# A mixture-of-experts kernel: experts of up to 64 tokens in a loop of their own, in plain float32 on two column groups

## Chip, cores and metric

One core of a Trainium2 chip. The metric is device time in microseconds for one execution, of the slowest core (here there is only one). Lower is better.

## What is computed

The kernel computes two transformer layers for 256 tokens of 1024 features, batch 1. The first layer has three attention branches; the second has a short convolution and a selecting attention, and then a mixture of experts, the part that matters here. With `t` the 256 tokens:

```python
scores = sigmoid(t @ w_router)                       # 256 x 64 experts
_, eidx = top_k(scores + router_bias, 8)             # 8 experts per token
g = take_along_axis(scores, eidx, axis=1)
g = g / sum(g, axis=-1) * 2.5
# for every expert e, over the tokens that chose it:
routed[tok] += (silu(t[tok] @ w1[e]) * (t[tok] @ w3[e])) @ w2[e] * g
out = routed + swiglu(t, ws1, ws3, ws2)
```

`w1` and `w3` are 1024 x 256 and `w2` 256 x 1024 for each of 64 experts, all float32: 2 MB for `w13` (w1 beside w3) and 1 MB for `w2` per expert. There are 256 x 8 = 2048 pairs of token and expert.

## The kernel before

Almost all matrix products keep float32 accuracy by splitting each operand into a high part that the fast float32 form (fp32r) holds exactly and a low part, and adding three products: high x high, low x high, high x low. The split costs one copy on ScalarE (high) and one subtraction on VectorE (low) per operand, weights included.

*Router* (`router`, L1324 to L1420). From the selection matrix `sel` (256 tokens x 64 experts) small products give the count per expert (`cnt`), a running start per expert and a slot number for each pair (`sg`, `sgT`), so that the 2048 slots hold the pairs sorted by expert. `nb` holds per expert whether it has a first block (count over 0.5) and a second one (over 128.5); `elist` lists, for each block, its expert and its first slot, `ecnt` the number of blocks. `place` (L1427) turns slot numbers into one-hot matrices. While the router's chain runs on VectorE, TensorE has the products of the shared expert.

*Gather* (`moe`, L1482 on). Four passes of 512 slots multiply the token rows with the one-hot matrices, so that `XT` holds the features of each slot and `ME` its expert weights and token number. The first blocks' weights are loaded and split meanwhile.

*The loop over blocks* (L1707 to L1755). A block is one expert with up to 128 slots, read at a start that is loaded into a register. Each iteration finishes block i - 1 and begins block i, with an order written out by hand for each engine:

- `stage_a(h, part)`: the first product, 128 slots as the stationary operand against w13 in halves h of 4 x 512 columns. Three products: 24 matmuls of 512 columns into `pa`.
- `silu`, `hidden`: silu(a) x b x gate into `ht`; `stage_t` transposes it in two pieces, `split_th` and `split_tl` split it.
- `stage_b(h)`: hidden x w2, three products: 12 matmuls of 512 columns into `py`; `split_yh` and `split_yl` split the result.
- `stage_c(h)`: adds the block's rows to their tokens, by a one-hot matrix `Q` (made from the token numbers by `token_distance` and `make_q`): 16 matmuls of 256 columns into the accumulators `acc`.
- `load_w` and `load_v`: six loads of 512 KB from SyncE's queue, for the next experts. SyncE first loads three expert numbers into registers.
- `split_wh`, `split_wl`, `split_vh`, `split_vl`: the splits of the weights on ScalarE, VectorE and, for one of them, GpSimd.

The loop runs from 1 to the number of blocks, which is known only at run time; the engines load it into registers (L1704). Behind the loop the last block is finished, the gate is applied and the output is stored (L1756 to L1775).

Of the kernel before, what the change touches and what calls it, by code (L numbers as in the profile page):

```python
# [20 lines left out]
S = 256  # L21
D = 1024
KD = 8
NE = 64
# [102 lines left out]
NSLOT = 2048  # L127
NB = 96
# [78 lines left out]
class Build:  # L207
# [1109 lines left out]
    def router(self, ps, lrow, r):  # L1317
        nc, a = self.nc, self.a
        rt = [self.s2("r"), self.s2("r"), self.s2("r", shape=(128, 512))]
        free = [r[:, t, s:s + 128].rearrange("p (a b) -> p a b", a=2) for r in rt[:2] for t in range(2) for s in (0, 128)]  # L1320
        w = lambda n: free.pop()
# [24 lines left out]
            nc.tensor.matmul(cps[:, 0:2], sel[:, qt, :], self.ones2, start=qt == 0, stop=qt == 1)  # L1346
        cnt = self.small([64, 2], F32, "cnt")
        nc.vector.tensor_copy(cnt, cps[:, 0:2])
        rk = self.pst([128, 2, NE], "O")
        nc.tensor.matmul(rk[:, 0, :], lt, sel[:, 0, :])  # L1350
        nc.tensor.matmul(rk[:, 1, :], self.ones2[:, 0:1].to_broadcast([128, 128]), sel[:, 0, :], start=True, stop=False)
# [13 lines left out]
        nb = self.small([64, 4], F32, "nb")  # L1365
# [4 lines left out]
        pps = self.pst([64, 4], "O")  # L1370
        nc.tensor.matmul(pps[:, 0:2], lt[0:64, 0:64], nb[:, 2:4])
        st = self.small([64, 4], F32, "st")
# [5 lines left out]
        self.places = [self.place(0)]  # L1378

        io = self.cm("iota")[0:64, 0:NB]  # L1380
        e1, e2 = rt[2][0:64, 0:NB], rt[2][0:64, 128:128 + NB]
        nc.vector.tensor_scalar(e1, io, st[:, 0:1], nb[:, 0:1], OP.is_equal, OP.mult)
        nc.vector.tensor_scalar(e2, io, st[:, 3:4], nb[:, 1:2], OP.is_equal, OP.mult)
# [12 lines left out]
        nc.tensor.matmul(nps, nb[:, 2:3], self.ones2[0:64, :])  # L1396
        self.ecnt = self.small([1, 2], I32, "ecnt")
        nc.vector.tensor_copy(self.ecnt, nps)
# [84 lines left out]
    def moe(self):  # L1483
# [4 lines left out]
        def tile(shape, dt, tag, bufs=1):  # L1488
            return mp.tile(shape, dt, tag=tag, name=tag, bufs=bufs)
# [116 lines left out]
        def meta_mm(b):  # L1606
            nc.tensor.matmul(pm[-1][:, 0:2], mslice, self.EB[:, bass.ds(b, 1), :].rearrange("p a b -> p (a b)"))
# [93 lines left out]
        nc.vector.tensor_scalar(zr, iota, 0.0, None, OP.mult)  # L1701
        for d2 in range(4):
            nc.tensor.matmul(acc2[d2], zr[:, 0:128], zr, start=True, stop=False, skip_group_check=True)
        n = nc.values_load(self.ecnt[0:1, 0:1], min_val=0, max_val=NB - 2)  # L1704


        with tc.For_i(1, n, 1, iteration_sync="reg_based") as iv:  # L1707
            with tc.manual_schedule():
# [44 lines left out]
                split_xl(1, s1)  # L1753
                load_w(0, e2, 0)
                split_wh(1, 1)  # L1755
        stage_t()  # L1756
        split_th()
        split_tl()
        token_distance()
        make_q()  # L1760
        for h in range(2):
            stage_b(h)
            split_yh(h)
            split_yl(h)
            stage_c(h)
# [29 lines left out]
```

## Time and profile before

| what | us |
|---|---|
| median of 3 runs | 998.45 (994.90 to 999.07) |
| the profiled execution | 997.92 |
| its span, from the first to the last instruction | 996.0 |
| TensorE busy (matmul) | 960.5 |
| VectorE busy | 809.0 |
| ScalarE busy | 599.9 |
| GpSimd busy | 162.2 |

Busy time counts the time in which at least one instruction of the engine was running. Matmuls overlap: one of 512 columns has a duration of 0.39 us, but the next one begins sooner; the distance of their starts is what one costs. The view by stretches gives for each engine its busy us and, in brackets, the number of instructions, then TensorE's granted clock (1.00 is full), the mean busy share of the 16 DMA engines, and what they moved. A timeline line gives start, duration, engine, line of the kernel, operation, what is written from what, shapes and how many instructions are merged into it; in square brackets stands how long the engine was idle before it and who ended that.

### The profile page before, as it was taken

How to read it: one execution, taken by the hardware profiler on the slowest of the kernel's cores; microseconds unless marked ns; L12 is line 12 of the kernel's file. 1: busy time of each engine (PE TensorE's matmuls, PEld its weight loads, DVE VectorE, ACT ScalarE, POOL GpSimd, SP SyncE). 2: the span in 40 equal slices, each digit the busy share in tenths (PEclk: the TensorE clock that was granted, in tenths of full speed). 3: DMA queues.
4: the chain of work that ended last, by engine and by line, in shares of the span. 5: the costliest groups of instructions: out<-in, count | busy, mean ns of one | idle time of the engine just before them, and what ended most of it. 6: DMA issues, size and time to landing. Idle time of an engine off the chain costs nothing. (4 is left out here: it accounts for less than half of the span.)

```text
span 996.0 us, 20282 instructions
## 1 busy us (share of the span) xinstructions
PE 960.5 (96%) x6666; PEld 884.2 (89%) x6666; DVE 809.0 (81%) x1479; ACT 599.9 (60%) x940; POOL 162.2 (16%) x111
## 2 busy tenths in 40 slices
PE   8999999999999999999898989999999999999996
PEld 7899999999999999999898977788888888888884
DVE  4777787777777758678874689799999999999994
ACT  5664654466355534555442535487887878878874
POOL 2311111011021000030200300021121221221211
PEclk9999999999999999999897989999999999999998
DMA  6576656676566465544330423388888888888884
GB/s 244 184 259 217 221 212 221 250 255 226 201 254 245 185 236 203 182 169 170 127 136 9 164 96 120 121 284 301 291 304 296 293 306 296 294 307 295 299 294 144
DMA packets 51209, 221.92 MB, mean 223 GB/s; under 512 B 5924, under 2 KB 6310, under 8 KB 41552
## 3 DMA queue, kind: packets, MB, share of 16 engines
q1 hardware_dynamic: 48960, 214.67, 60.9%
q0 software_dynamic: 1760, 5.42, 2.0%
q10 hardware_dynamic: 432, 1.05, 0.3%
q8 instruction: 38, 0.62, 0.3%
q14 instruction: 19, 0.16, 0.0%
HBM read 220.01 MB, written 1.11 MB: 222 GB/s over the span
## 5 line engine op out<-in xcount | busy, mean ns | idle before, releaser
L249 ACT ACTIVATE wh<-raw 128x2048 fp32r<-128x2048 f32 x75 | 143.5, 1914 | 108.5 <-DMA raw<-w_in 79.7
L250 DVE TENSOR_TENSOR raw<-raw,wh 128x2048 fp32r<-128x2048 f32 x75 | 171.5, 2287 | 14.8 <-ACT wh L249 14.6
L1536 ACT ACTIVATE wh<-raw 128x1024 fp32r<-128x1024 f32 x136 | 139.6, 1055 | 59.7 <-PE mm L1561 47.9
L329 PE MATMUL mm<-wh,hH 128*128 128x256 f32 x448 | 128.5, 287 | 0.0
L1545 POOL TENSOR_TENSOR raw<-raw,wh 128x1024 fp32r<-128x1024 f32 x32 | 77.0, 2407 | 302.3 <-PE mm L1561 302.3
L331 PE MATMUL mm<-wh,hL 128*128 128x256 f32 x448 | 125.9, 281 | 0.0
L330 PE MATMUL mm<-raw,hH 128*128 128x256 f32 x448 | 125.8, 281 | 0.0
L1560 PE MATMUL mm<-wh,xH 128*128 128x512 f32 x264 | 105.8, 401 | 0.0
L329 PE MATMUL mm<-hH,wh 128*128 128x256 f32 x352 | 103.1, 293 | 0.0
L1561 PE MATMUL mm<-wh,xL 128*128 128x512 f32 x264 | 103.0, 390 | 0.0
L331 PE MATMUL mm<-hH,raw 128*128 128x256 f32 x352 | 100.4, 285 | 0.9 <-DVE raw L250 0.9
L330 PE MATMUL mm<-hL,wh 128*128 128x256 f32 x352 | 99.9, 284 | 0.0
L329 PEld LDWEIGHTS mm<-wh,hH 128*128 128x128 f32 x448 | 84.5, 189 | 1.5
L330 PEld LDWEIGHTS mm<-raw,hH 128*128 128x128 f32 x448 | 84.5, 189 | 0.2 <-DVE raw L250 0.2
L331 PEld LDWEIGHTS mm<-wh,hL 128*128 128x128 f32 x448 | 84.4, 188 | 0.1
L1539 DVE TENSOR_TENSOR raw<-raw,wh 128x1024 fp32r<-128x1024 f32 x68 | 79.8, 1211 | 0.0
L1539 DVE TENSOR_TENSOR WL<-raw,wh 128x1024 fp32r<-128x1024 f32 x66 | 79.8, 1210 | 0.0
L598 DVE CUSTOM_DVE_ANT_0 ada<-ada,silc 128x1024 f32<-128x1024 f32 x48 | 58.6, 1221 | 24.9 <-DMA ada<-w_ada 24.9
L406 POOL TENSOR_TENSOR hr<-hss,mhalf 128x8 f32<-128x8 f32 (+2 forms) x24 | 41.8, 1743 | 169.0 <-DVE hss L405 168.8
L329 PEld LDWEIGHTS mm<-hH,wh 128*128 128x128 f32 x352 | 67.4, 191 | 1.1
L331 PEld LDWEIGHTS mm<-hH,raw 128*128 128x128 f32 x352 | 66.9, 190 | 1.2 <-DVE raw L250 1.2
L330 PEld LDWEIGHTS mm<-hL,wh 128*128 128x128 f32 x352 | 67.6, 192 | 0.0
(510 smaller groups left out, 2586.4 us busy)
## 6 DMA issues: line engine op xcount, KB each, us to landing
raw<-w SPq DMA_DIRECT2D x204, 512.0 KB, 5.4
raw<-w_in SPq DMA_DIRECT2D x58, 1024.0 KB, 4.8
ada<-w_ada SPq DMA_DIRECT2D x48, 512.0 KB, 5.8
raw<-w_out SPq DMA_DIRECT2D x8, 1024.0 KB, 4.7
raw<-w_branch SPq DMA_DIRECT2D x6, 1024.0 KB, 4.7
tb<-rext POOLq DMA_DIRECT2D x20, 256.0 KB, 4.7
raw<-ws SPq DMA_DIRECT2D x3, 1024.0 KB, 4.9
out<-x SPq DMA_DIRECT2D x4, 256.0 KB, 2.3
```

The source lines that it names most:

```text
L249: h = nc.scalar.activation(hi, raw, AF.Copy)
L250: l = nc.vector.tensor_tensor(lo, raw, hi, OP.subtract)
L329: nc.tensor.matmul(out, lh, rh, start=start, stop=False)
L330: nc.tensor.matmul(out, lh, rl, start=False, stop=False)
L331: self.last_mm = nc.tensor.matmul(out, ll, rh, start=False, stop=stop).ins
L406: nc.gpsimd.tensor_tensor(r, ss, self.mhalf[:, 0:2 * nh], OP.pow)
L598: nc.vector.tensor_tensor_reduce(raw, raw, self.silc, 0.5, 0.0, OP.mult, OP.add, self.ada[:, m:m + 1])
L1536: nc.scalar.activation(WH[h][:, half(p)], rw[h][:, half(p)], AF.Copy)
L1539: nc.vector.tensor_tensor(WL[h][:, half(p)], rw[h][:, half(p)], WH[h][:, half(p)], OP.subtract)
L1545: (nc.vector, nc.gpsimd)[f].tensor_tensor(VL[f], rw2[f], VH[f], OP.subtract)
L1560: nc.tensor.matmul(pa, xH[h][:, k, :], WH[h][:, ws], start=h == 0 and k == 0, stop=False)
L1561: nc.tensor.matmul(pa, xL[h][:, k, :], WH[h][:, ws], start=False, stop=False)
```

## The change

Experts with more than 64 tokens come first, in the first loop, which is as before. Those with 1 to 64 tokens come behind them in a second loop, two of them per iteration. There the weights are used as they are loaded, as plain float32, without a split. The stationary operand is 64 slots wide; the columns of w13 and of w2 are taken in two halves, one written to partitions 0 to 63 of the result and one to 64 to 127. The result of stage b lies in these two halves, so that stage c multiplies 64 rows at a time. The loads are 1 MB each instead of 512 KB. The router counts large and small experts and numbers the slots with the large ones first; the block that did the counting stands earlier. `ecnt` now holds the number of large blocks (at least 1) and the end of the second loop, and a second register load per engine reads it.

In the router (cut):

```diff
+        nc.vector.tensor_scalar(nb[:, 1:2], cnt[:, 0:1], 64.5, None, OP.is_gt)
+        nc.vector.scalar_tensor_tensor(q[:, 0:1], cnt[:, 0:1], 128.5, nb[:, 1:2], OP.is_gt, OP.add)
+        nc.vector.tensor_tensor(q[:, 1:2], cnt[:, 0:1], nb[:, 1:2], OP.mult)
+        nc.vector.scalar_tensor_tensor(q[:, 2:3], cnt[:, 0:1], 0.5, nb[:, 1:2], OP.is_gt, OP.subtract)
+        nc.vector.tensor_tensor(q[:, 3:4], cnt[:, 0:1], q[:, 1:2], OP.subtract)
+        pps = self.pst([64, 4], "O")
+        nc.tensor.matmul(pps, lt[0:64, 0:64], q, start=True, stop=False)
+        nc.tensor.matmul(pps[:, 2:4], self.ones2[0:64, 0:1].to_broadcast([64, 64]), q[:, 0:2], start=False, stop=True)
+        nc.vector.tensor_copy(pp, pps)
+        nc.vector.tensor_tensor(pp[:, 0:2], pp[:, 0:2], pp[:, 2:4], OP.subtract)
+        nc.vector.scalar_tensor_tensor(st[:, 0:2], pp[:, 0:2], nb[:, 1:2], pp[:, 2:4], OP.mult, OP.add)
...
-        nc.tensor.matmul(sb_ps, cnt[:, 0:1].to_broadcast([64, 128]), lt[0:64, 0:64])
+        nc.tensor.matmul(sb_ps, st[:, 1:2].to_broadcast([64, 128]), self.vec("ident")[0:64, 0:64])
...
-        nc.vector.tensor_scalar(nb[:, 0:1], cnt[:, 0:1], 0.5, None, OP.is_gt)
-        nc.vector.tensor_scalar(nb[:, 1:2], cnt[:, 0:1], 128.5, None, OP.is_gt)
-        nc.vector.tensor_tensor(nb[:, 2:3], nb[:, 0:1], nb[:, 1:2], OP.add)
-        nc.vector.tensor_copy(nb[:, 3:4], cnt[:, 0:1])
-        nc.tensor.matmul(pps[:, 0:2], lt[0:64, 0:64], nb[:, 2:4])
-        nc.vector.tensor_copy(st[:, 0:2], pps[:, 0:2])
```

The loops' bounds, and the products of the new loop (`part` are the partitions 0 to 63 and 64 to 127):

```diff
-        n = nc.values_load(self.ecnt[0:1, 0:1], min_val=0, max_val=NB - 2)
+        n = nc.values_load(self.ecnt[0:1, 0:1], min_val=1, max_val=NB - 16)
+        n_end = nc.values_load(self.ecnt[0:1, 1:2], min_val=1, max_val=NB - 16)
...
+        def s_a(pn, h, first, last):
+            w = W13[pn][h].rearrange("p (k g t c) -> p k g t c", k=4, g=2, t=2)
+            for k in range(4):
+                for t in range(2):
+                    nc.tensor.matmul(pa[part[t], 0:256], xs[pn][:, 4 * h + k, :], w[:, k, :, t, :],
+                                     start=first and k == 0, stop=last and k == 3)
...
+        def s_b(pn):
+            for f in range(2):
+                for t in range(2):
+                    c = 1024 * f + 512 * t
+                    nc.tensor.matmul(py[0][part[t], :], tS[pn][:, 64 * f:64 * f + 64], W2[pn][:, c:c + 512],
+                                     start=f == 0, stop=f == 1)
+
+        def s_c(pn):
+            for d in range(4):
+                ds = slice(128 * d, 128 * d + 128)
+                for y, last in ((yH[0], False), (yL[0], True)):
+                    for t in range(2):
+                        nc.tensor.matmul(acc[4 * t + d], y[part[t], ds], Qs[pn][part[t], :], start=False, stop=last,
+                                         skip_group_check=True)
```

One turn of the new loop (finishes expert i, begins i + 1), the piece between the loops, and the second loop. `s_load13` and `s_load2` issue the loads of 1 MB, `s_slot` loads a start slot into a register of VectorE, `s_x` copies 64 slots of `XT`, `s_meta` the weight and token numbers, `s_q` makes `Q`, `s_t` transposes the hidden values and `s_ts` copies them:

```diff
+        def s_turn(pc, i=None):
+            pn = 1 - pc
+            if i is not None:
+                e3, e2, s = expert(i + 3), expert(i + 2), s_slot(i + 2)
+            s_ts(pc)
+            s_a(pn, 0, True, False)
+            s_q(pn)
+            if i is not None:
+                s_load13(pn, 0, e3)
+                s_x(pc, i + 2, s)
+            s_b(pc)
+            split_yh(0)
+            if i is not None:
+                s_load2(pc, e2)
+            split_yl(0)
+            s_a(pn, 1, False, True)
+            if i is not None:
+                s_load13(pn, 1, e3)
+                s_meta(pc, i + 2)
+            s_silu()
+            s_hidden(pn)
+            s_c(pc)
+            s_t()
...
+            s_load13(0, 0, e0)
+            s_load2(0, e0)
+            s_load13(1, 1, e1)
+            s_load2(1, e1)
+            stage_t()
+            split_th()
+            split_tl()
...
+            s_a(0, 1, True, False)
+            s_load13(0, 1, e2)
+            stage_b(0)
...
+            stage_b(1)
...
+            stage_c(0)
+            stage_c(1)
+            s_a(0, 0, False, True)
+            s_load13(0, 0, e2)
+            s_silu()
+            s_q(0)
+            s_hidden(0)
...
+            s_t()
+        with tc.For_i(n, n_end, 2, iteration_sync="reg_based") as iv:
+            with tc.manual_schedule():
+                s_turn(0, iv)
+                s_turn(1, iv + 1)
+        with tc.manual_schedule():
+            s_turn(0)
+            s_ts(1)
+            s_b(1)
+            split_yh(0)
+            split_yl(0)
+            s_c(1)
```

The first loop's last iteration has already loaded one half of w13 for the first small expert and one for the second; the new loop takes these buffers over. The buffers of the split weights serve as the other float32 weight buffers.

## Rows read from the trace of the kernel before

**Rows 1.** The page: busy time of the engines, and the loads of the block loop.
```profile
PE 960.5 (96%) x6666; PEld 884.2 (89%) x6666; DVE 809.0 (81%) x1479; ACT 599.9 (60%) x940; POOL 162.2 (16%) x111
...
raw<-w SPq DMA_DIRECT2D x204, 512.0 KB, 5.4
```

**Rows 2.** Stretches: 50 us inside the block loop, and the last 16 us.
```profile
core 0: us, PE busy (x) PEld busy (x) DVE busy (x) ACT busy (x) POOL busy (x), PEclk, DMA share, GB/s
...
700.00:750.00 50.00, 50.00 (x270) 43.34 (x269) 48.97 (x73) 39.44 (x56) 12.04 (x5) 1.00 0.87 300
...
980.00:996.00 16.00, 8.40 (x30) 6.31 (x30) 3.86 (x8) 3.75 (x8) 2.17 (x3) 0.72 0.18 66
```

**Rows 3.** Timeline of SyncE's queue: the w13 loads of the last two iterations.
```profile
959.79 4.12 SPq L1504 DMA_DIRECT2D raw<-w  x4
...
970.32 4.12 SPq L1504 DMA_DIRECT2D raw<-w  x4
```

**Rows 4.** Timeline of TensorE inside one iteration: 512 columns, then 256.
```profile
805.93 1.08 PE L1563 MATMUL mm<-WL,xH 128*128 128x512 f32 x4
...
807.42 0.28 PE L1601 MATMUL S<-Q,hL 128*128 128x256 f32 x1
807.54 0.28 PE L1600 MATMUL S<-Q,hH 128*128 128x256 f32 x1
```

**Rows 5.** Timeline of TensorE in the second layer's attention: float32 on two row groups.
```profile
462.59 0.28 PE L331 MATMUL mm<-wh,hL 128*128 128x256 f32 x1
...
462.80 0.49 PE L1196 MATMUL S<-ki,qi 64*128 64x256 f32 x2
...
463.12 0.39 PE L1196 MATMUL S<-ki,qi 64*128 64x256 f32 x2
463.34 0.28 PE L1197 MATMUL S<-ki,qi 64*128 64x128 f32 x2
```

**Rows 6.** Groups of instructions by line and shape, 680 to 996 us: VectorE and ScalarE.
```profile
L1551 DVE TENSOR_SCALAR xH<-XT 128x512 fp32r x57 | 41.2, 723 | 0.0
...
L1595 DVE TENSOR_TENSOR hL<-O,hH 128x512 fp32r<-128x512 f32 x30 | 20.2, 674 | 0.0
L1592 ACT ACTIVATE hH<-O 128x512 fp32r<-128x512 f32 x29 | 17.4, 599 | 10.6 <-PE O L1589 10.6
...
L1569 DVE SCALAR_TENSOR_TENSOR ht<-th,meta,mm 128x256 f32<-128x256 f32 x29 | 13.9, 481 | 4.7 <-ACT th L1566 2.8
...
L1566 ACT ACTIVATE th<-mm 128x256 f32<-128x256 f32 x29 | 11.1, 383 | 6.2 <-PE mm L1563 6.1
```

**Rows 7.** Stretches: loads queued up at the start, and in the block loop.
```profile
7.50:15.00 7.50, 6.80 (x41) 6.31 (x42) 5.01 (x9) 6.07 (x13) 0.00 (x0) 0.77 1.01 410
...
954.00:956.50 2.50, 2.50 (x22) 2.42 (x21) 2.34 (x5) 1.97 (x4) 2.10 (x1) 1.00 0.99 395
940.00:970.10 30.10, 30.10 (x163) 26.09 (x162) 29.64 (x44) 23.69 (x35) 7.22 (x3) 1.00 0.87 292
```

**Rows 8.** Waits and timeline of TensorE at the loop's entry and exit.
```profile
PE O L1575 <- PEq L1707: 1.1, 1, 1.1
...
980.99 0.66 PE L1575 MATMUL O<-vecs,ht 128*128 128x128 f32 x2 [3.30 <-PEq L1784]
...
983.17 0.63 PE L1586 MATMUL mm<-wh,tH 128*128 128x512 f32 x1
...
987.30 0.39 PE L1589 MATMUL O<-raw,tH 128*128 128x512 f32 x1
...
989.93 0.28 PE L1601 MATMUL T<-Q,hL 128*128 128x256 f32 x1
```

**Rows 9.** Timeline of VectorE and TensorE in the router: count, slot starts, first slot product.
```profile
580.66 0.15 DVE L1348 COPY cnt<-O 64x2 f32<-64x2 f32 x1 [0.16 <-PE O L1346]
...
581.53 0.43 PE L1356 MATMUL O<-cmat,cnt 64*128 64x64 f32 x2
...
585.27 1.19 PE L1439 MATMUL O<-hH,sgT 64*128 64x512 f32 x2 [2.35 <-DVE mtH L1409]
```

More of the change, by code (lines that the diff above doesn't have):

```diff
@@ L1348, in router @@
         nc.vector.tensor_copy(cnt, cps[:, 0:2])
+        nb = self.small([64, 4], F32, "nb")
+        q = self.small([64, 4], F32, "nq")
+        nc.vector.tensor_scalar(nb[:, 1:2], cnt[:, 0:1], 64.5, None, OP.is_gt)
[6 more added lines that the diff above has]
+        nc.tensor.matmul(pps[:, 2:4], self.ones2[0:64, 0:1].to_broadcast([64, 64]), q[:, 0:2], start=False, stop=True)
+        pp = self.small([64, 4], F32, "pp")
+        nc.vector.tensor_copy(pp, pps)
+        st = self.small([64, 4], F32, "st")
+        nc.vector.tensor_tensor(pp[:, 0:2], pp[:, 0:2], pp[:, 2:4], OP.subtract)
+        nc.vector.scalar_tensor_tensor(st[:, 0:2], pp[:, 0:2], nb[:, 1:2], pp[:, 2:4], OP.mult, OP.add)
         rk = self.pst([128, 2, NE], "O")
@@ L1364, in router @@
         nc.scalar.activation(self.sgT, gps, AF.Copy)
-        nb = self.small([64, 4], F32, "nb")
-        nc.vector.tensor_scalar(nb[:, 0:1], cnt[:, 0:1], 0.5, None, OP.is_gt)
-        nc.vector.tensor_scalar(nb[:, 1:2], cnt[:, 0:1], 128.5, None, OP.is_gt)
-        nc.vector.tensor_tensor(nb[:, 2:3], nb[:, 0:1], nb[:, 1:2], OP.add)
-        nc.vector.tensor_copy(nb[:, 3:4], cnt[:, 0:1])
-        pps = self.pst([64, 4], "O")
-        nc.tensor.matmul(pps[:, 0:2], lt[0:64, 0:64], nb[:, 2:4])
-        st = self.small([64, 4], F32, "st")
-        nc.vector.tensor_copy(st[:, 0:2], pps[:, 0:2])
         nc.vector.tensor_tensor(st[:, 2:3], st[:, 1:2], cnt[:, 0:1], OP.add)
@@ L1378, in router @@
         self.places = [self.place(0)]
+        nc.vector.tensor_scalar(nb[:, 0:1], cnt[:, 0:1], 0.5, None, OP.is_gt)
+        nc.vector.tensor_scalar(nb[:, 2:3], cnt[:, 0:1], 128.5, None, OP.is_gt)
         io = self.cm("iota")[0:64, 0:NB]
@@ L1382, in router @@
         nc.vector.tensor_scalar(e1, io, st[:, 0:1], nb[:, 0:1], OP.is_equal, OP.mult)
-        nc.vector.tensor_scalar(e2, io, st[:, 3:4], nb[:, 1:2], OP.is_equal, OP.mult)
+        nc.vector.tensor_scalar(e2, io, st[:, 3:4], nb[:, 2:3], OP.is_equal, OP.mult)
         p2 = self.small([64, 4], F32, "p2")
@@ L1395, in router @@
         nps = self.pst([1, 2], "O")
-        nc.tensor.matmul(nps, nb[:, 2:3], self.ones2[0:64, :])
+        nc.tensor.matmul(nps, self.ones2[0:64, 0:1], q.rearrange("p (a b) -> p a b", b=2)[:, :, 0])
         self.ecnt = self.small([1, 2], I32, "ecnt")
-        nc.vector.tensor_copy(self.ecnt, nps)
+        en = self.small([1, 4], F32, "en")
+        nc.vector.tensor_copy(en[:, 0:2], nps)
+        nc.vector.tensor_tensor(en[:, 3:4], en[:, 0:1], en[:, 1:2], OP.add)
+        nc.vector.tensor_scalar(self.ecnt[:, 0:1], en[:, 0:1], 1.0, None, OP.max)
+        nc.vector.tensor_scalar(self.ecnt[:, 1:2], en[:, 3:4], -2.0, 1.0, OP.add, OP.max)
         nc.vector.tensor_tensor(G, sel, sa, OP.mult)
@@ L1755, in moe @@
                 split_wh(1, 1)
[L1756 to L1765, printed above, removed]
+        wh = self.turn["wh"]
+        f32t = lambda i: self.wp.tile([128, 2048], F32, tag=f"wh_{(wh + i) % 3}", name="wf", bufs=1)
+        W13 = [[f32t(1), rw[1]], [rw[0], f32t(2)]]
+        W2 = [rv, mp.tile([128, 2048], F32, tag="WL1", name="wf", bufs=1)]
@@ new lines, in moe, with s_load13 @@
+        xs = [tile([128, 4, 128], F32, f"xH{i}").rearrange("p a (b c) -> p (a b) c", b=2) for i in range(2)]
+        Qs = [Q, tile([128, 4, 128], F32R, "xL0")[:, 0:2, :].rearrange("p a b -> p (a b)")]
+        meta2 = [tile([128, 2], F32, f"meta2{i}") for i in range(2)]
+        tSS = tile([128, 2, 128], F32, "tH")
+        tS = [tSS[:, i, :] for i in range(2)]
+        ms = mslice
+        part = (slice(0, 64), slice(64, 128))
+        def s_load13(pn, h, e):
+            nc.sync.dma_start(W13[pn][h], a["w13"][bass.ds(e, 1), :, 2048 * h:2048 * h + 2048].rearrange("a p n -> p (a n)"))
@@ new lines, in s_load2, with expert, s_slot, s_x @@
+        def s_load2(pn, e):
+            nc.sync.dma_start(W2[pn], a["w2"][bass.ds(e, 1), :, :].rearrange("a p n -> p (a n)"))
+        def expert(i):
+            return nc.sync.value_load(self.elist[0:1, 0, bass.ds(i, 1)], min_val=0, max_val=NE - 1)
+        def s_slot(i):
+            return nc.vector.value_load(self.elist[0:1, 1, bass.ds(i, 1)], min_val=0, max_val=NSLOT)
+        def s_x(pn, i, s):
+            nc.vector.tensor_scalar(xs[pn], XT[:, :, bass.ds(s, 64)], 1.0, None, OP.mult)
+            for j in range(2):
+                nc.vector.tensor_scalar(ms[:, 64 * j:64 * j + 64], ME[:, bass.ds(s, 64)], 1.0, None, OP.mult)
@@ new lines, in s_meta, with s_q @@
+        def s_meta(pn, i):
+            meta_mm(i)
+            nc.vector.tensor_copy(meta2[pn], pm[-1][:, 0:2])
+        def s_q(pn):
+            nc.scalar.activation(pm[-1][:, 256:512], iota[:, 0:S], AF.Abs, bias=meta2[pn][:, 1:2], scale=-1.0)
+            nc.scalar.activation(Qs[pn], pm[-1][:, 256:512], AF.Relu, bias=1.0, scale=-1.0)
+        def s_a(pn, h, first, last):
[4 more added lines that the diff above has]
+                                     start=first and k == 0, stop=last and k == 3)
@@ new lines, in s_silu, with s_hidden, s_t, s_ts @@
+        def s_silu():
+            nc.scalar.activation(th[:, 0:128], pa[:, 0:128], AF.Silu)
+        def s_hidden(pn):
+            nc.vector.scalar_tensor_tensor(ht[:, 0:128], th[:, 0:128], meta2[pn][:, 0:1], pa[:, 128:256], OP.mult, OP.mult)
+        def s_t():
+            nc.tensor.transpose(py[1][:, 0:128], ht[:, 0:128], self.vec("ident"))
+        def s_ts(pn):
+            nc.vector.tensor_copy(tS[pn], py[1][:, 0:128])
+        def s_b(pn):
[4 more added lines that the diff above has]
+                                     start=f == 0, stop=f == 1)
@@ new lines, in moe @@
+        with tc.manual_schedule():
+            e0, e1, e2 = (expert(n + i) for i in range(3))
+            s0, s1 = (s_slot(n + i) for i in range(2))
+            s_load13(0, 0, e0)
[5 more added lines that the diff above has]
+            split_tl()
+            token_distance()
+            make_q()
+            s_x(0, n, s0)
+            s_meta(0, n)
+            s_a(0, 1, True, False)
[4 more added lines that the diff above has]
+            stage_b(1)
+            split_yh(1)
+            split_yl(1)
+            stage_c(0)
[5 more added lines that the diff above has]
+            s_hidden(0)
+            s_x(1, n + 1, s1)
+            s_meta(1, n + 1)
+            s_t()
@@ L1766, in moe @@
+        with tc.For_i(n, n_end, 2, iteration_sync="reg_based") as iv:
+            with tc.manual_schedule():
+                s_turn(0, iv)
+                s_turn(1, iv + 1)
+        with tc.manual_schedule():
+            s_turn(0)
+            s_ts(1)
+            s_b(1)
+            split_yh(0)
+            split_yl(0)
+            s_c(1)
         for p in range(KD // 2):
```

## The prediction, made before the changed kernel was run

> **What bounds the kernel now.** I read the page first, then stretches, then the loop over expert blocks, because the change lies in it. The page [rows 1] gives TensorE busy for 960.5 us, 96% of the span. The stretches [rows 2] show where room is left: in 700 to 750 us TensorE is busy 50.00 of 50 us at full clock and VectorE 48.97, while the DMA engines are busy 87% and move 300 GB/s; at the end (980 to 996) TensorE is busy only half the time and at a mean clock of 0.72. So the loop is bound by TensorE, with VectorE close behind; the loads are third.
>
> One iteration takes 10.53 us (the distance of the groups of w13 loads in [rows 3]). That is a sum of matmuls [rows 4]: 36 of 512 columns (four in a row take 1.08 us where one alone takes 0.39, so they start 0.23 us apart) and 16 of 256 columns (807.42 to 807.54, 0.12 us apart): 8.3 + 1.9 = 10.2 us, and two transposes and the meta product make up the rest. All of this is done for 128 slots, whatever the expert's own count.
>
> The trace doesn't show the counts. Evaluating the reference's router on its inputs gives 33 experts with tokens: 17 with 69 to 124, 16 with 1 to 59, none above 128. The trace agrees on the 33: 204 loads of 512 KB [rows 1] are 34 experts of 3 MB, one more than 33 because the loop loads ahead. So the first loop keeps 16 of its 32 iterations, 16 experts go to the new loop, and 16 x 10.53 = 168.5 us are taken out.
>
> **The change, part by part.** *TensorE in one turn of the new loop.* A float32 matmul is recorded as two matmuls. In [rows 5] two float32 matmuls of 64 rows and 256 columns stand side by side on the two row groups: the first two records begin at 462.80 and end within 0.49 us; the second two begin together at 463.12, and the next line begins at 463.34. So a record of 256 columns takes 0.22 us (463.12 to 463.34), a whole matmul 0.43 us, and the two groups run at the same time. The change pairs by columns instead: both halves read the same 128 partitions and write partitions 0 to 63 and 64 to 127. No row shows such a pair. Bounds: as parallel as the row groups (0.43 us a pair of 256 columns), or one after the other (0.86). I take the first, by the nearest rows, which are those row pairs. Then stage a is 8 pairs x 0.43 = 3.46 us, stage b 2 pairs of 512 columns x 0.86 = 1.73 us. Stage c is 16 matmuls of 64 rows in 8 pairs on row groups: 8 x 0.12 = 0.96 us (1.9 if they don't pair). The transpose and the two meta records take 0.35 us. Four times a turn the array changes its division; 462.59 to 462.80 [rows 5] is 0.21 us where 0.12 is usual, so 0.1 us each, and I take 0.6 us in all (0.4 to 1.2). Sum 7.1 us; ends 6.9 to 8.6.
>
> Nothing else in a turn is that long. VectorE has one 512-element copy (0.72 us), one split of y (0.67), the product (0.48) and four small ones, under 3 us; ScalarE has the y copy (0.60), silu (0.38) and the two for Q, under 2 us [rows 6]. All weight splits disappear. The chain stage a, silu, hidden, transpose costs 0.38 + 0.48 us and two handovers, some 1.1 us; it lies beside the meta product and stage c (1.4 us with the array changes), so I cost it at nothing; if that cover is gone it is 0.5 us a turn. The y splits (1.3 us) lie under the second half of stage a (1.73). On SyncE two register loads stand ahead of three issues, where one iteration had three ahead of six and kept up [rows 3]; a load is asked for over a turn before its use, so those queued behind a wait there have time. On VectorE the new register load stands ahead of the copy of the transposed hidden; stage b, which waits for that copy, has half a stage a (1.73 us) before it. I add 0.6 us a turn for waits that don't fit: **7.7 us a turn**.
>
> *Loads.* From the end of the first loop to the last w2 that is needed, 47 loads of 1.05 MB are issued: 49.3 MB. In the first loop 292 GB/s move at a share of 0.87 [rows 7], which would be 336 at a share of 1. Where the queue is backed up it is more: 410 GB/s in 7.5 to 15 us, with rows of 8 KB as the new loop has, and 395 GB/s for 2.5 us inside the loop [rows 7]. I take 385. The first new issue comes at about 979.5 us on the old time axis (the loop's last group of w13 is issued at 970.32 to 974.4 [rows 3]; then the loop's exit and three register loads). With 2 us to begin, the last w2 lands at 981.5 + 49.3 / 0.385 = 1109.5. TensorE asks for it at 1116.6 (below), so the loads are just covered; they end last below 49.3 / 135.1 = 365 GB/s. The Trainium skill gives a limit of about 358 GB/s of HBM bandwidth per core (DMA: Bandwidth & Descriptors, section Specifications). By it the loads would end last by 2.6 us and the sum would be 964; the 410 GB/s of [rows 7] speak against it.
>
> *The seams.* When the loop ends, TensorE stands still for 3.3 us, and then runs at half clock for some 6 us: a matmul of 512 columns takes 0.63 us at 983.17 and 0.39 again at 987.30 [rows 8], which is 0.43 against 0.23 us from one to the next. The change has two loops, so this comes twice; a loop's entry costs 1.1 us [rows 8]. Between the loops TensorE does, from 981.0 on: transposes 0.7, meta 0.4, half a stage a at half clock 3.5, 12 matmuls of stage b 3.3 (three of them at half clock), stage c 2.2 with its wait, the other half of stage a 1.7, silu, hidden and transpose uncovered 1.5, entry 1.1: 14.4 us. After the second loop: exit 3.3, the last turn 7.1 and 3.0 for the half clock, then stage b 1.7, y 1.3, stage c and array changes 1.2: 17.6 us. Before, the piece from 981.0 to the last matmul at 990.2 was 9.2 us [rows 8]; the output behind it is unchanged.
>
> *The router.* The block that counts large and small experts now stands ahead of the slot numbers. Five dependent VectorE operations of about 0.15 us (as the copy of the count), two small products and three more VectorE operations come between the count (580.66) and the product at 581.53 [rows 9]; the four operations and the product that stood later go. TensorE stands still 2.35 us before 585.27, waiting at the end of this VectorE chain [rows 9], so nothing covers what is added. Bounds: 0.5 us less (the later block is gone) to 2 us more; I take 0.9 us, by the length of the five operations, which is the nearest row. The second register load for the loop's end adds 0.5 us. Together 1.4 us.
>
> **Sum.** New: 14.4 + 14 x 7.7 + 17.6 = 139.8 us. Gone: 168.5 + 9.2 = 177.7 us. Difference 37.9, less 1.4: 36.5 us. Against the profiled execution (997.92 us, near the median of 998.45) that is **961 us**.
>
> **The rivals.** (a) *The column halves don't run side by side.* For it: both streams read the same 128 partitions, while those of [rows 5] read 64 each; a float32 record streams its operand for twice as long as a record of the split kind, so the way by which it comes in may not have room for two. Against it: a record of 256 columns takes 0.22 us, twice the 0.12 us of [rows 4], so one stream alone takes in columns at half the rate that those matmuls reach. Price: stages a and b double, 5.2 us a turn; the turn then has no slack and is 12.6 us; 14 x 4.9 + 13.9 for the seams and the last turn on top: **1044 us**. It decides from a pair that takes 1.45 times one matmul on (36.5 us over 16 turns is 2.3 us of 5.2): beyond that the change is slower.
> (b) *They overlap in part.* A pair that takes 1.25 times one matmul adds 1.3 us a turn, some 22 us in all: **983 us**. The Trainium skill gives 2.38 times for three column groups side by side (TensorE: Matmul & The Clock Gate, Part 3), where full overlap would be 3; an estimate from that page is a stretch of 1.26 and 984 us. No run here shows it.
> (c) *The loads stay at the rate they have now.* At 292 GB/s the last w2 lands at 1150, 34 us after it is wanted: **995 us**; at 336 GB/s it is 973 us. For it: the loop was never waiting for them, so nothing shows it sustained. Against it: [rows 7].
> (d) *The clock.* TensorE's clock fell to half after it stood still [rows 8]; if the waits of the new loop did that throughout, a turn would be over 14 us and the result over 1060 us. The waits that I expect are all under 1.5 us.
> That the change doesn't do what it says would mean fewer small experts than 16; each one fewer costs 2.8 us.
>
> **How the numbers follow.** Forecast with its own range of 947 to 974 us (a turn of 7.0 to 8.6 us, the seams 3 us better or worse): 0.70. Partial overlap, 974 to 1000 us: 0.10. Loads at the old rate: 0.04. Serial halves: 0.14. Clock: 0.02. The range 947 to 996 holds nearly all of the first, most of the second and the third: 0.8. A measurement of this kernel tells about 0.5% from no change (993 to 1003 us). Faster: the forecast, most of (b) and a little of (c), 0.80; same 0.05; slower 0.15.
>
> **What would show it.** After the change the first loop should have 16 iterations at 10.5 us. In the second, two float32 records of stage a should begin within some 0.02 us of each other, and pairs follow every 0.22 us; 0.22 us per single record would be rival (a). A turn should be 7 to 8.5 us; if TensorE's waits in it name the weights as what it waited for, the loads end last and their rate tells (c). After each loop there should be a pause of about 3 us and a half clock behind it. The router's wait before the first slot product should be within 2 us of 2.35. Wrong would be above all a different number of turns, or a pair that isn't one.

## The result, and the profile after

| what | us |
|---|---|
| before, median of 4 runs | 998.06 (994.90 to 999.07) |
| after, median of 4 runs | 966.39 (964.21 to 969.38) |
| ratio | 0.968, 95% interval 0.966 to 0.970 |
| after, the profiled execution | 969.38 |
| its span | 967.6 |

The change makes the kernel 31.7 us faster. Predicted were 961 us (947 to 996).

The page of the changed kernel, the lines that answer to [rows 1]:

```profile
PE 915.5 (95%) x6716; PEld 816.6 (84%) x6716; DVE 675.8 (70%) x1359; ACT 492.6 (51%) x812; POOL 124.0 (13%) x95
...
raw<-w SPq DMA_DIRECT2D x108, 512.0 KB, 5.2
wf<-w SPq DMA_DIRECT2D x25, 1024.0 KB, 10.0
...
raw<-w SPq DMA_DIRECT2D x23, 1024.0 KB, 9.6
```

The weight loads that were 204 of 512 KB are now 108 of 512 KB, 18 experts (17 large ones and one loaded ahead), and 48 of 1 MB. So the counts are as the prediction had them: 16 experts moved to the new loop. Each of the new loads needs 10 us from its issue to its landing, where those before needed 5.4 [rows 1]: the queue is backed up. The stretches show the same (columns as in [rows 2]):

```profile
700.00:750.00 50.00, 50.00 (x264) 43.12 (x263) 49.24 (x73) 39.89 (x58) 11.30 (x5) 1.00 0.89 299
...
860.00:900.00 40.00, 40.00 (x342) 24.73 (x340) 11.88 (x42) 10.44 (x24) 0.00 (x0) 1.00 1.01 422
900.00:930.00 30.00, 30.00 (x252) 17.93 (x248) 8.07 (x29) 6.95 (x16) 0.00 (x0) 1.00 1.01 422
930.00:945.00 15.00, 4.79 (x41) 2.85 (x37) 1.14 (x3) 0.88 (x2) 0.00 (x0) 0.71 0.99 414
945.00:967.00 22.00, 11.79 (x81) 6.59 (x81) 4.37 (x10) 3.65 (x8) 2.12 (x3) 0.81 0.14 50
```

The first loop (700 to 750) is as it was. In the second (860 to 930) TensorE is busy without a gap at full clock, VectorE and ScalarE have little to do, and the DMA engines are full: 422 GB/s at a share of 1.01. Both limits are reached at once. Then come 15 us with TensorE idle for 10 of them, while the loads go on at 414 GB/s, and a tail at a mean clock of 0.81. A gap of that size is the one large thing that the prediction did not have.

One turn of the new loop on TensorE, from the timeline (columns as in [rows 4]):

```profile
858.67 1.89 PE L1832 MATMUL mm<-wf,tH 128*64 128x512 f32 x8
860.39 1.90 PE L1813 MATMUL mm<-raw,xH 128*64 128x256 f32 x16
862.22 0.38 PE L1620 MATMUL O<-EB,mslice 66*128 x2
862.53 0.38 PE L1840 MATMUL S<-xL,hH 64*128 64x256 f32 x1
862.53 0.38 PE L1840 MATMUL T<-xL,hH 64*128 64x256 f32 x1
...
863.68 0.33 PE L1823 MATMUL O<-vecs,ht 128*128 128x128 f32 x1
863.93 1.95 PE L1813 MATMUL mm<-raw,xH 128*64 128x256 f32 x16
865.71 1.89 PE L1832 MATMUL mm<-raw,tH 128*64 128x512 f32 x8
```

Stage b (L1832) begins at 858.67 and again at 865.71: a turn of 7.04 us. Half a stage a (L1813) is 8 matmuls, recorded as 16; they take 860.39 to 862.22, 1.83 us, so two records every 0.23 us. Taken record by record (the single records behind a merged line), the two column groups begin 0.007 us apart, and pairs follow every 0.216 us. Stage c (L1840) shows its row pairs openly: two records at 862.53.

The seams, from the same timeline:

```profile
817.58 0.66 PE L1588 MATMUL O<-vecs,ht 128*128 128x128 f32 x2 [3.05 <-PEq L1929]
...
819.79 0.56 PE L1620 MATMUL O<-EB,mslice 66*128 x2 [1.56 <-DVE mslice L1799]
...
832.60 0.35 PE L1620 MATMUL O<-EB,mslice 66*128 x2 [1.39 <-DVE mslice L1799]
...
834.21 3.51 PE L1813 MATMUL mm<-raw,xH 128*64 128x256 f32 x16 [1.09 <-ACT O L1806]
...
934.67 0.33 PE L1823 MATMUL O<-vecs,ht 128*128 128x128 f32 x1
946.74 3.52 PE L1813 MATMUL mm<-raw,xH 128*64 128x256 f32 x16 [11.74 <-PEq L1929]
...
955.50 1.94 PE L1832 MATMUL mm<-wf,tH 128*64 128x512 f32 x8 [0.38 <-DVE tH L1826]
```

The first loop ends with a pause of 3.05 us, like the 3.30 of [rows 8]. The second ends with one of 11.74 us: the last turn in the loop is over at 935.0, and TensorE, VectorE and ScalarE begin again together at 946.72 to 946.74. What follows runs at half clock first (granted clock 0.50 from 946.7 to 950.0; 3.52 us for 16 records that take 1.90 inside the loop).

What TensorE waits for is not named: "PEq" is its own sequencer. The waits of SyncE's queue name it. First 930 to 960 us of the changed kernel, then its first loop's end (805 to 820), then the loop's end of the kernel before (960 to 985), a row that I had not read (columns: who waits and for whom, us in total, times, longest):

```profile
SPq L1900 <- DMA wf<-w: 7.3, 3, 2.5
SPq L1900 <- DMA raw<-w: 4.5, 2, 2.4
```

```profile
SPq L1721 <- DMA raw<-w: 3.4, 3, 1.4
```

```profile
SPq L1707 <- DMA raw<-w: 4.0, 3, 1.5
```

L1900, L1721 and L1707 are the lines of the loops themselves. At a loop's end SyncE waits for each load that is still in flight, and no engine goes on before SyncE does. Behind the second loop these are five loads, with a landing every 2.48 us (1.05 MB at 422 GB/s): 7.3 + 4.5 = 11.8 us, the length of TensorE's pause. Before, it was three shorter waits for loads of 512 KB, 4.0 us; record by record the last of these loads is seen at 980.34, SyncE is through at 980.9, and TensorE begins at 980.99 [rows 8]. The pause that I took for a fixed price of a loop's end was already mostly a wait for loads.

### The profile page after: what moved, and what is told of

Read it like the earlier page. It is cut to its first block, busy times and chain, and to the rows that moved or that the text cites. A ratio compares the mean times of both kernels' runs of the same rounds, so it can differ in the third digit from the quotient of the medians.

```text
span 967.6 us, 19260 instructions
## 1 busy us (share of the span) xinstructions
PE 915.5 (95%) x6716; PEld 816.6 (84%) x6716; DVE 675.8 (70%) x1359; ACT 492.6 (51%) x812; POOL 124.0 (13%) x95
## 3 DMA queue, kind: packets, MB, share of 16 engines
q10 hardware_dynamic: 432, 1.05, 0.3%
## 5 line engine op out<-in xcount | busy, mean ns | idle before, releaser
L331 PE MATMUL mm<-hH,raw 128*128 128x256 f32 x352 | 100.8, 286 | 1.6 <-DVE raw L250 1.6
L1549 ACT ACTIVATE wh<-raw 128x1024 fp32r<-128x1024 f32 x72 | 73.6, 1055 | 35.0 <-PE mm L1574 28.3
L1608 DVE TENSOR_TENSOR hL<-mm,hH 128x512 fp32r<-128x512 f32 x33 | 22.5, 683 | 62.3 <-ACT hH L1605 62.3
L1558 POOL TENSOR_TENSOR raw<-raw,wh 128x1024 fp32r<-128x1024 f32 x16 | 38.6, 2412 | 171.2 <-PE mm L1574 171.2
L490 ACT ACTIVATE sp<-sp,am 128x256 f32<-128x256 f32 x96 | 42.3, 443 | 27.1 <-DVE am L470 27.1
L1573 PE MATMUL mm<-wh,xH 128*128 128x512 f32 x136 | 54.4, 400 | 0.0
L1574 PE MATMUL mm<-wh,xL 128*128 128x512 f32 x136 | 53.1, 391 | 0.0
```

Of the source, the lines that this page charges most:

```text
L331: self.last_mm = nc.tensor.matmul(out, ll, rh, start=False, stop=stop).ins
L490: nc.scalar.activation(p, p, AF.Exp, bias=m[:, qt, G - 1:G], scale=-1.0, accum_out=s[:, half, qt, g:g + 1])
L1549: nc.scalar.activation(WH[h][:, half(p)], rw[h][:, half(p)], AF.Copy)
L1558: (nc.vector, nc.gpsimd)[f].tensor_tensor(VL[f], rw2[f], VH[f], OP.subtract)
L1573: nc.tensor.matmul(pa, xH[h][:, k, :], WH[h][:, ws], start=h == 0 and k == 0, stop=False)
L1574: nc.tensor.matmul(pa, xL[h][:, k, :], WH[h][:, ws], start=False, stop=False)
```

## The experiments

The theory after the result: (1) the column groups run at the same time, and because of that a turn is 7.05 us; (2) the pause behind the second loop is the backlog of loads; (3) the large loads hold 422 GB/s, and this just covers TensorE; (4) so the change has a fixed price for its seams and a gain per small expert. Each was set against a rival. The kernel before ran beside the experiments at 997.93 to 999.84 us, as the median of each call.

**Same column group.** Both halves go to partitions 0 to 63, added up there:

```diff
-                    nc.tensor.matmul(pa[part[t], 0:256], ...
-                                     start=first and k == 0, stop=last and k == 3)
+                    nc.tensor.matmul(pa[same[t], 0:256], ...
+                                     start=first and k == 0 and t == 0, stop=last and k == 3 and t == 1)
...
-                    nc.tensor.matmul(py[0][part[t], :], ...
+                    nc.tensor.matmul(py[0][same[t], :], ...
```

> The changed kernel with one edit: both column halves of stages a and b of the small experts go to partitions 0 to 63, so to one column group, and are added up there (so the output of these experts is not the wanted one; the work, its operands and its order are the same). Nothing can run side by side in these two stages. The theory, that the two column groups give a factor of two in these stages, expects that a pair of records of 256 columns then takes 0.43 us where it takes 0.216, a turn 7.05 + 3.46 + 1.73 = 12.2 us, that the loads then have slack and the wait at the second loop's exit falls below 4 us, and in all 966 + 14 x 5.2 + 12 (the piece between the loops, the last turn) - 8 (the exit) = about 1043 us, slower than the kernel before. The rival, that one column group alone takes in the next matmul early enough to hide part of it, expects turns of 8 to 10 us and 980 to 1010 us.

Measured: 1038.2 us (one run), a turn of 12.2 us. Its timeline of TensorE, and the wait at the second loop's exit:

```profile
860.99 3.60 PE L1833 MATMUL mm<-raw,tH 128*64 128x512 f32 x8
864.42 3.62 PE L1814 MATMUL mm<-wf,xH 128*64 128x256 f32 x16
867.97 0.38 PE L1620 MATMUL O<-EB,mslice 66*128 x2
```

```profile
PE mm L1814 <- PEq L1930: 4.4, 1, 4.4
```

The same 16 records take 864.42 to 867.97, 3.55 us instead of 1.83, and the turn is 5.15 us longer, of which 5.2 were expected. This is the price that the prediction gave for serial halves (1044 us), here in a run. So the second column group is worth 5.15 us a turn and decides the sign of the whole change: without it the kernel is 40 us slower than before. With a turn of 12.2 us the loads have slack, and the exit's pause falls to 4.4 us.

**No pairs in the order.** The two halves of stages a and b stand one behind the other instead of alternating:

```diff
-            for k in range(4):
-                for t in range(2):
+            for t in range(2):
+                for k in range(4):
```

(and in stage b the loops over `f` and `t` likewise)

> The two column halves of stages a and b are issued one after the other (all matmuls to partitions 0 to 63, then all to 64 to 127), same arithmetic. Theory (halves run side by side when they are issued in turn, 0.22 us per pair of records): pairs disappear, each turn gets 5.2 us longer (7.05 to 12.2 us), the loads then have slack and the wait at the second loop's exit falls from 11.7 to about 4 us; in all about 79 us more than the changed kernel, 1045 us. Rival (the records only look paired, the array works on one at a time): order makes no difference, 966 us.

Measured: 979.26 us (one run), a turn of 8.1 us: neither. Its timeline of TensorE:

```profile
857.82 2.21 PE L1813 MATMUL mm<-wf,xH 128*64 128x256 f32 x13
859.66 0.64 PE L1832 MATMUL mm<-wf,tH 128*64 128x512 f32 x1
859.87 0.59 PE L1813 MATMUL mm<-wf,xH 128*64 128x256 f32 x2
860.14 0.59 PE L1832 MATMUL mm<-wf,tH 128*64 128x512 f32 x1
860.30 0.38 PE L1813 MATMUL mm<-wf,xH 128*64 128x256 f32 x1
860.51 1.45 PE L1832 MATMUL mm<-wf,tH 128*64 128x512 f32 x5
```

Stage a (L1813) and stage b (L1832), which follow each other in the program, are mixed here. Record by record, the second group's first matmul begins at 858.736, when three of the eight records of the first group are still to come, and the first group's last one begins at 859.378 (which group a record belongs to is told by its distance to the next, 0.216 us). So by the profile's start times TensorE takes matmuls of the other column group ahead of those that are still waiting for their own, but not without limit: 1.03 us of the possible 5.15 is lost a turn. The pairs come from the column groups; the order only has to keep the two halves near each other. Fifteen turns of 1.03 us are 15.5 us; the exit's pause is 3.6 us shorter, since the loads have more time, and 966.4 + 15.5 - 3.6 = 978 fits the 979:

```profile
PE mm L1813 <- PEq L1929: 8.1, 1, 8.1
```

**No loads in the loop.** All loads inside the second loop are left out:

```diff
-                e3, e2, s = expert(i + 3), expert(i + 2), s_slot(i + 2)
+                s = s_slot(i + 2)
...
-                s_load13(pn, 0, e3)
...
-                s_load2(pc, e2)
...
-                s_load13(pn, 1, e3)
```

> The loads inside the second loop are left out (the experts from the 20th on are computed with weights of the experts before them). Theory (a turn is bound by TensorE, the exit by loads in flight): turns stay at 7.05 us, the exit falls from 11.7 us to 3 us or less; 957 us. Rival (turns are bound by the loads): turns fall below 6.8 us, 952 us or less.

Measured: 951.09 us (one run). The exit of its second loop, from the timeline of TensorE:

```profile
928.69 0.33 PE L1823 MATMUL O<-vecs,ht 128*128 128x128 f32 x1
929.54 1.95 PE L1813 MATMUL mm<-raw,xH 128*64 128x256 f32 x16 [0.53 <-PEq L1925]
```

Without loads the pause is 0.53 us where it was 11.74, and no half clock follows (1.95 us for the 16 records). The turns stay at 7.04 us: inside the loop the loads cost TensorE only some 0.6 us, in the last two turns (7.19 and 7.47 us in the changed kernel). The turn around the exit takes 7.3 us instead of 20.1, 12.8 us. So the mechanism is the theory's; its size is larger than I expected, because the half clock went with the pause. That the total is at 951 and not at 969.38 - 12.8 = 956.6 has a cause ahead of the change: the profiled execution of the changed kernel reaches the first loop some 5 us later than this one (its first block's transpose stands at 645.6 us, here at 640.6).

**Written out.** The second loop's 14 turns are written out for this input's counts, so there is no second loop, and the two loads that nobody uses are left out (diff cut):

```diff
-        with tc.For_i(n, n_end, 2, iteration_sync="reg_based") as iv:
-            with tc.manual_schedule():
-                s_turn(0, iv)
-                s_turn(1, iv + 1)
         with tc.manual_schedule():
+            for i in range(17, 31):
+                s_turn((i - 17) % 2, i)
             s_turn(0)
```

> The second loop's 14 turns are written out one after the other for this input's counts, and the two loads that nobody uses (w13 of a 34th expert) are left out; no loop exit between the turns. Theory (at the exit of a loop SyncE waits until every load in flight has landed, and all engines wait for SyncE; the weights that the next turn needs are there already): the 11.7 us at the exit and about 1 us of the half clock behind it disappear, 954 us. Rival (the last weights end last anyway, the exit only shows it): only the 5 us of the two unused loads are saved, 961 us.

Measured: 952.39 us (951.25 to 954.30), ratio 0.952 (0.951 to 0.954). The end of its turns, from the timeline of TensorE:

```profile
929.39 1.95 PE L1813 MATMUL mm<-raw,xH 128*64 128x256 f32 x16 [0.18 <-DMA raw<-w]
...
936.84 1.95 PE L1813 MATMUL mm<-wf,xH 128*64 128x256 f32 x16 [0.19 <-DMA wf<-w]
```

All loads are there, at 420 GB/s, and TensorE waits 0.2 us for two of them. So the 11.74 us behind the loop were no need of the computation: the weights for the last turn were there in time, and only the loop's end asked for more. This run takes away the loop's end and the two unused loads (5 us of the queue) together; the run with late loads, next, has no unused loads but keeps the loop, and its pause is still 5.8 us. Relative to the kernel before, this version is 15.8 us faster than the changed kernel (47.5 against 31.7). From 20.1 to 7.1 us around the exit is 13.0 us of it, and 9.7 to 7.0 in the first turn, without the loop's entry and its half clock, is 2.7; one of its turns takes 8.1 us and gives 1.1 back (TensorE waits 0.82 us for VectorE's split there; why in this turn alone, I don't know). It is the fastest version that does all the work, but for these counts alone: the number of turns is fixed in the program.

**Late loads.** The w13 of the expert after next is asked for at the turn's start, into the buffer that has just come free, instead of one turn ahead in halves; so there are fewer loads in flight, and none that nobody uses:

```diff
-                e3, e2, s = expert(i + 3), expert(i + 2), s_slot(i + 2)
+                e2, s = expert(i + 2), s_slot(i + 2)
+                s_load13(pc, 0, e2)
+                s_load13(pc, 1, e2)
...
-                s_load13(pn, 0, e3)
...
-                s_load13(pn, 1, e3)
```

> w13 of expert i + 2 is asked for at the beginning of turn i instead of w13 of expert i + 3 in its course, so that at the exit only loads that are used are in flight, and fewer. Theory (the exit waits for what is in flight): the exit falls from 11.7 to about 6 us, turns grow from 7.2 to at most 7.5 us since they now wait for loads at 422 GB/s; 962 to 966 us. Rival (prefetch over two turns is needed): turns of 8 us and more, over 972 us.

Measured: 965.27 us (964.76 to 966.27), ratio 0.966 (0.964 to 0.968). Its waits of TensorE:

```profile
PE mm L1813 <- PEq L1927: 5.8, 1, 5.8
```

The pause is halved, and the gain is given back: the turns are 7.0 us at first and 7.4 to 7.5 from the seventh on. 3.15 MB a turn at 423 GB/s (its 860 to 900 us) are 7.4 us; so without a lead the loads end last, by 0.4 us. In the changed kernel the lead built up between the loops pays for this difference, and it is nearly used up at the end: its last turns inside the loop are 7.2 and 7.5 us. TensorE and the loads are that close.

**Half loads.** The loads of the second loop are 512 KB (rows of 4 KB) instead of 1 MB (rows of 8 KB), twice as many:

```diff
-            nc.sync.dma_start(W2[pn], ...
+            for j in range(2):
+                c = 1024 * j
+                nc.sync.dma_start(W2[pn][:, c:c + 1024], ...
```

(and each half of w13 likewise)

> Each load of 1 MB of the second loop becomes two of 512 KB, with rows of 4 KB as in the first loop. Theory (the rate is set by how many loads are queued, not by their size): at least 400 GB/s, the exit's wait grows by 1 to 3 us, 966 to 970 us. Rival (the first loop's 299 GB/s come from the small rows): 48 loads take some 40 us longer, about 1000 us.

Measured: 977.03 us (976.11 to 977.86), ratio 0.977 (0.975 to 0.979). Its stretches, and its waits of TensorE from 860 us on:

```profile
860.00:900.00 40.00, 38.88 (x328) 23.22 (x326) 11.35 (x42) 9.84 (x23) 0.00 (x0) 1.00 1.00 386
900.00:930.00 30.00, 26.95 (x205) 14.38 (x202) 6.64 (x22) 5.81 (x13) 0.00 (x0) 1.00 1.00 364
```

```profile
PE mm L1819 <- PEq L1935: 14.1, 1, 14.1
PE mm L1819 <- DMA wf<-w: 2.0, 6, 0.6
PE mm L1838 <- DMA raw<-w: 1.7, 3, 0.8
```

At a share of 1.00 the engines now move 386 and 364 GB/s where they moved 422. The loss is not spread evenly: by issue and landing, 38 of the 49 distances between landings from 860 to 930 us are at most 1.32 us, 1.28 in the middle, which is 410 GB/s; the other eleven, 1.36 to 3.02 us, hold the rest. SyncE, too, works differently here, since with twelve loads per iteration it waits for earlier landings before it issues the first of them, and the others follow in a burst:

```profile
SPq L1787 <- DMA wf<-w: 26.6, 12, 4.5
```

My theory, that the rate comes from the number of queued loads alone, falls: between 860 and 930 three to eight are in flight, and in the changed kernel three to six, and its last loads still land 2.5 us apart with two and one left. The rival's 1000 us falls as well, since it took the rate inside the first loop, 292 GB/s at a share of 0.87 [rows 7], which is 336 at a full share. In this experiment the turns stretch to between 7.6 and 9.4 us once the lead is used up, and the exit's pause to 14.1. I changed the size of a load and the length of its rows together, and with them the moments of issue; which of the three counts stays open.

**Other limits.** With the limit at 2.5 tokens, 4 experts are small and 29 go through the first loop; with 50.5, 14 are small and 19 large. One constant in the router changes:

```diff
-        nc.vector.tensor_scalar(nb[:, 1:2], cnt[:, 0:1], 64.5, None, OP.is_gt)
+        nc.vector.tensor_scalar(nb[:, 1:2], cnt[:, 0:1], 2.5, None, OP.is_gt)
```

> Limit 2 instead of 64 tokens: 4 experts in the second loop (one iteration of it), 29 blocks in the first. With the seams as the changed kernel's trace shows them (some 22 us) and 3.35 us gained per small expert: 998 + 22 - 13 = 1006 us. With the seams as predicted (8.8 us) and 2.8 us per expert: 996 us.

> Limit 50 instead of 64 tokens: 14 experts in the second loop, 19 blocks in the first. With 3.35 us gained per small expert, as the turns of the changed kernel's trace show: 6.7 us more than with limit 64, 973 us. With the predicted 2.8 us: 972 us. If the exit's wait grew with the number of turns, less: 969 us.

Measured: with 4 small experts 1005.44 us (1002.04 to 1007.12), ratio 1.0057 (1.0035 to 1.0079), so 0.6% slower than before; with 14, 973.08 us (970.38 to 974.32), ratio 0.974 (0.972 to 0.976), which can't tell the expected 973 from 972. The exit's pause on TensorE, for 4 and for 14:

```profile
PE mm L1813 <- PEq L1929: 7.5, 1, 7.5
```

```profile
PE mm L1813 <- PEq L1929: 11.7, 1, 11.7
```

Against the kernel before of the same call, 4 small experts give +6.0 us, 14 give -26.4 and 16 give -31.7. An iteration of 10.55 us that becomes a turn of 7.05 is worth 3.5 us. By that the seams cost 6.0 + 4 x 3.5 = 20.0 us, 22.6 and 24.3, each with about 2 us either way: 22.6 and 24.3 can't be told apart, and the 20.0 goes with the shorter backlog at the loop's end (7.5 us where it is 11.7 for 14 and 16). With few small experts the change loses; it breaks even near 20 / 3.5, about 6 of them.

## Why the prediction was right, and where it was not

**Bound and count.** Right: 16 iterations of 10.55 us remain and 16 experts moved. The forecast of 961 was 5 us short of 966, and two errors of opposite sign stand behind it.

**The turn.** The step from the row pairs of [rows 5] to column pairs was right. Pairs follow every 0.216 us (I took 0.22), and the sum of 7.1 us for TensorE is the 7.04 measured. The 0.6 us that I added for waits didn't come: VectorE, ScalarE and SyncE were as far off as their rows said. Fourteen turns took 834.21 to 935.0, 100.8 us, where I had 107.8. The evidence for the pairing itself is the run with one column group: it turned the pair of 0.22 us into 0.44, and 966 us into 1038, close to the 1044 of rival (a). Rival (b), partial overlap, was wrong for this order of matmuls. A loss of its size appeared when the order was changed (8.1 us a turn, 979 us, where I had 983), but from another cause, halves that stand too far apart in the program. The Trainium skill (TensorE: Matmul & The Clock Gate, Part 3) has 2.38 times for three column groups; here two groups gave 3.55 / 1.83 = 1.94, array change included.

**The loads.** 385 GB/s was too low: 422. Rival (c), 292, had no part in it. The step that held was to read the rate where a queue was backed up with rows of mostly 8 KB, 410 GB/s [rows 7]; I then gave too much weight to the 395 inside the loop, whose loads are half as large. The run with half loads moved 364 to 386 in the place of 422, for a reason that stays open. The Trainium skill (HBM Reference, Specifications (TRN2)) says that a core streaming alone reaches about 425 GB/s, and that 358 is the share when both cores of a pair stream; the trace agrees with the first. The loads "just covered", as the prediction had them, is what the run with late loads shows, by 0.4 us a turn.

**The seams.** This is the term that was mis-sized. I took 3.3 us for the second loop's exit, from the first loop's [rows 8]; it was 11.74. The number was read correctly and its cause wasn't looked up: the waits of SyncE at L1707 would have told that most of these 3.3 us is loads in flight. The prediction's own text then had what was needed, loads backed up and landing until after TensorE's last turn; from these follow five loads of 2.5 us behind the loop. With the loads taken out the pause was 0.53 us, and with the loop written out nothing was left of it. The rest of the tail, half clock and last turn, was close: 935.0 to the last matmul's end at 960.0 are 25 us, 11.7 for the pause and 13.3 for the rest, where I had 14.3.

The piece between the loops took 16.6 us (817.58 to 834.21) where I had 14.4: TensorE waits 1.56 and 1.39 us for the copy of the token numbers (`mslice`, L1799), which stands behind the copy of the features (`s_x`, L1797) on VectorE. The second stands where I had 1.5 us for the handovers; the first stood in no term. The 1.09 us before 834.21 is the second loop's entry, for which I had 1.1: the profile names a ScalarE operation that ends at 834.02, but record by record TensorE's own sequencer is busy with the loop's registers and branch until 833.98. Behind these waits came one half clock more than the sum had: the granted clock is 0.50 from 833.9 to 837.3, the 16 records from 834.21 take 3.51 us where 1.90 is usual, and the first turn 9.7 us where the others take 7.0. In the turns that followed the clock of rival (d) did not fall.

**The router.** Right for the step that was priced, but it doesn't show in the time to the loop. The copy of the count and the first slot product of the changed kernel:

```profile
585.95 0.15 DVE L1348 COPY cnt<-O 64x2 f32<-64x2 f32 x1 [0.16 <-PE O L1346]
...
591.42 1.19 PE L1452 MATMUL O<-hH,sgT 64*128 64x512 f32 x2 [1.07 <-DVE hH L1447]
```

That is 5.47 us, where [rows 9] give 4.61 (580.66 to 585.27): 0.86 us more, and I took 0.9. The first transpose of the loop, before and after:

```profile
640.37 0.43 PE L1575 MATMUL O<-vecs,ht 128*128 128x128 f32 x2 [1.05 <-PEq L1707]
```

```profile
645.60 0.43 PE L1588 MATMUL O<-vecs,ht 128*128 128x128 f32 x2 [0.40 <-issue]
```

It begins 59.71 us after the count before [rows 9] and 59.65 us after it now. Behind the slot product the gather is as much shorter, 54.18 us where it was 55.10: the middle distance of its matmuls of 512 columns is 0.227 us in all nine traces with the new loop and 0.232 in the one of the kernel before. Why, stays open. The 0.5 us for the second register load stood on no row, and nothing of it is seen either.

**The sum.** New 16.6 + 100.8 + 25.0 = 142.4 us, where I had 139.8; so the turns' 7.0 us too much hid 2.2 us too little between the loops and 7.4 too little behind them. By the prediction's own terms the difference would be 168.8 + 9.2 - 142.4 - 1.4 = 34.2 us. Two of them are to be corrected: the 1.4 us of the router don't show in the time to the loop, and "the output behind it is unchanged" does not hold. From the last matmul's end to the end of the span the kernel before takes 5.8 us (990.2 to 996.0) and the changed one 7.6 (960.0 to 967.6). Before, the output of the first four feature blocks began while TensorE still had half of stage c; now all accumulators are finished in one stage c. The first operation of the output, before and after:

```profile
988.09 0.48 DVE L1770 SCALAR_TENSOR_TENSOR x<-S,ada,x 128x256 f32<-128x256 f32 x1 [1.65 <-PE S L1601]
```

```profile
959.51 0.48 DVE L1915 SCALAR_TENSOR_TENSOR x<-S,ada,x 128x256 f32<-128x256 f32 x1 [0.71 <-PE T L1840]
```

With that the difference is 168.6 + 9.2 - 142.4 - 1.8 = 33.6 us (the 16 iterations, from the loop's first transpose to its exit, are 168.6). The two profiled spans differ by 996.0 - 967.6 = 28.4 us, because the changed kernel's execution, the longest of its four, is 5.3 us behind already at the count (580.66 and 585.95), ahead of all changed code: 28.4 + 5.3 = 33.7, so the sum closes. In the profiled executions of the experiments the count lies anywhere between 580.8 and 585.7 us. The medians, of other executions too, give 31.7 us with about 2 us either way.

The two errors offset each other only at this count. As a formula in the number N of small experts, the prediction was 8.8 - 2.83 N us; the runs give about 20 to 24 - 3.5 N. At 16 these differ by 5 us. At 4 the prediction gives -2.5 and the run +6.0: the other sign. One total that fits doesn't show that its terms do.

## What to carry to other kernels

A pause at a loop's end is not a constant: look up in SyncE's waits which loads are in flight there, multiply their number by the time between two landings, and ask again for the new loop, above all where the change makes it short of bandwidth. When a price is taken over from one place to another, take over the row that names its cause, not only its length. Two plain float32 matmuls of 64 columns of the stationary operand that write different halves of the partitions cost here as much as one, if they alternate in the program; check it by sending both to the same half.

## What the runs showed of the hardware

- At the end of this kernel's loops, whose count is known only at run time, all engines stand until the loads in flight have landed: 11.74 us with five 1 MB loads, 5.8 with fewer in flight, 0.53 without. TensorE then begins at half clock after 11.74 us, and at full clock after 0.53.
- Loads of 1 MB in rows of 8 KB moved 422 GB/s over 70 us with the DMA engines full; loads of 512 KB in rows of 4 KB moved 386 and 364 in the same stretches, with most landings at the pace of 410 and a few late ones.
- TensorE starts matmuls of one column group ahead of earlier ones that wait for the other group, by three records of 256 columns in the run in blocks: there a turn was 8.1 us, in pairs 7.04, on one group 12.2.
